# Hybrid encoder on one core: one more feed-forward chunk as seven products, shared PSUM banks, wider weight sums, and x kept in DRAM during the FFN

## The chip, the cores and the metric

The kernel runs on one core of one Trainium2 chip, in one launch. The metric is device time in microseconds (us), lower is better. The kernel before was run three times: 1098.07, 1098.73 and 1100.32 us, median 1098.73 us. One further execution was profiled; it took 1098.06 us. Engine names are those of the profile: PE (TensorE matmuls), PEld (its weight loads), DVE (VectorE), ACT (ScalarE), POOL (GpSimd), SP (SyncE, here a queue of DMA issues).

## What is computed

A residual trunk of two layers on 512 tokens of width 1024, all in float32. Layer 0 mixes tokens by a bidirectional gated linear attention (GLA), layer 1 by grouped-query softmax attention; each is followed by a gated feed-forward network (FFN) with a depthwise convolution of width 3 over the tokens:

```python
for i in range(DEPTH):
    h = rmsnorm(x, norm_mix[i])
    x = x + (gla_mixer(h, ...) if i % 2 == 0 else attn_mixer(h, ...))
    x = x + conv_ffn(rmsnorm(x, norm_ffn[i]), ...)

def conv_ffn(h, w_up, w_conv, b_conv, w_down):
    u = h @ w_up                                # 512 x 1024 by 1024 x 5632
    u = depthwise_conv_width_3(u, w_conv) + b_conv
    val, gate = split(u, 2)
    return (silu(gate) * val) @ w_down          # 512 x 2816 by 2816 x 1024
```

The change is in the FFN, which runs twice with the same code, and in what the FFN shares with the rest (temporaries, x).

## The kernel before, in words

**Layout.** x is held transposed, as eight tiles of 128 features by 512 tokens. Every matrix product in full precision is three float32r matmuls: a number is split into a high part (its rounding to float32r, by a copy on ACT) and a low part (the rest, by a subtraction on DVE), and high*high, high*low and low*high are added up in PSUM. So each 128x1024 weight piece costs one ACT copy (L227) and one DVE subtraction (L228) beside its load; activations are split in the same way. Where a tile is split "by DMA" (`low_dma`, L178) ACT makes both the high part and the negated high part, and a DMA of POOL's queue (L217, in `flush`) adds the original to it, so that DVE has nothing to do.

**Weights.** `Weights` holds the list of all pieces in the order of use (`todo`). `piece` hands out one and makes the next ones ahead of use, `UPA` or `PA` pieces (3 and 4); `make` splits a piece into a `wh` and a `wl` tile, of which there are four each (`NH`, `NL`), and `load` issues the DMA on SP into one of four `raw` tiles, `LOADS` (3) keys ahead.

**The up-projection** runs over 22 chunks m; each gives 128 features of val (t=0) and 128 of gate (t=1). A plain chunk (`plain_up`) has two tiles of 8 x 3 = 24 matmuls of 512 columns (L387 to L389 under `mm3`), 48 in all. The chunks of `SEVEN` (twelve of them: 7, 8, 10-13, 15, 16, 18-21) treat the chunk as a 2x2 block product (inputs even/odd k, tokens in two halves of 256) by seven instead of eight block products (a Strassen-Winograd scheme). A block product is 4 pairs x 3 = 12 matmuls of 256 columns (L857), so a chunk has 84. `seven_up` writes out the order of the products and of the ACT copies and DVE additions between them: product 1 goes to r1; ACT copies r1 to r2 (L873), product 6 adds to r2; ACT copies r2 to r3 (L877), products 7, 3, 5 and 4 follow, then product 1 of the next chunk (`begin_up`), then product 2. The results go to SBUF temporaries c and d of tag `u` by L885 to L894. Four weight quarters are loaded per such chunk and combined by `summed` into seven operands in four pieces; `PLACE` says which piece holds which product's weight.

**The convolution** (`act_up`, L904 to L909) takes one ACT and two DVE passes per tile, then silu and the product. In the first `SWITCH` (4) chunks the input is only scaled by the norm's weight, and a DVE pass per tile (L845) multiplies by the row norms R; after that the inputs are `fresh`, eight tiles rescaled by `rescale` and split by DMA. The sums and differences of the inputs for the seven products are made by `prepare_input` after the chunks in `INPUT_AT`.

**The down-projection.** Every two chunks `prepare` makes the seven inputs of one pair p for the down product (q, differences, then four splits into `gu` tiles); for p in `Q_DMA` (2, 4, 5, 6) the splits go by DMA. After chunks 9 and 17 (`DOWN_AFTER`) `down_part` multiplies eight chunks by their down weights, again by seven products for each of four output pairs n; its results f and g are added to x in SBUF by DMAs of POOL's queue. The last six chunks follow at the end as plain matmuls ("dn"), and `end` adds them to x on DVE (L1008).

**Order.** Each engine runs its instructions in the order in which the tile framework's planner has put them, which follows the program's order where operands and buffers are ready by its own estimate of times. A tile of a tag waits until one of that tag's buffers is free. PSUM has eight banks: acc 3, s 2, pt 2, po 1.

Of the kernel before, what the change touches and what calls it, by code (L numbers as in the profile page):

```python
# [48 lines left out]
SEVEN = (7, 8, 10, 11, 12, 13, 15, 16, 18, 19, 20, 21)  # L49
# [3 lines left out]
SWITCH = 4  # L53
INPUT_AT = {3: (0, 1), 4: (2,), 5: (3,)}
Q_DMA = (2, 4, 5, 6)
NR = 4
NH = 4
NL = 4

# [9 lines left out]
def hybrid_encoder_kernel(  # L69
# [25 lines left out]
    pp = ctx.enter_context(tc.tile_pool(name="pp", bufs=1, space=bass.MemoryType.PSUM))  # L95

# [17 lines left out]
    def tmp(tag, n, w=S):  # L114
        return sp.tile([P, w], F32, tag=tag, bufs={"u": 4, "t": 6, "sq": 3}[tag], name=nm(n))
# [5 lines left out]
    x = [cp.tile([P, S], F32, name=f"x{c}") for c in range(KC)]  # L121
    prm = cp.tile([P, PC_N], F32, name="prm")

    class Weights:
# [3 lines left out]
        def __init__(self):  # L128
            self.todo, self.made, self.by_dma, self.pending = [], {}, [], []
            self.sums, self.last, self.fine = set(), None, []  # L130
            self.loaded, self.strip = {}, {}

        def add(self, src, strips=None, pieces=2):
            for i in strips or range(src.shape[0]):
                order = (0, 1, 3, 2) if pieces > 2 and src.shape[0] == FC else range(pieces)
                self.todo += [(src, i, h) for h in order]
                if pieces > 2:
                    self.sums.add((id(src), i))
# [22 lines left out]
        def make(self, key):  # L161
# [7 lines left out]
            if any(src is a and i < n for a, n in self.by_dma):  # L169
                self.low_dma(hi, lo, r)  # L170
            else:
# [3 lines left out]
        def two(self):  # L175
            return pair("wh", NH, F32R, "wh"), pair("wl", NL, F32R, "wl")

        def low_dma(self, hi, lo, r):  # L178
            act.activation(hi, r, AF.Copy)
            act.activation(lo, r, AF.Copy, scale=-1.0)  # L180
            self.pending.append((lo, r))

        def summed(self, src, i, h):
# [3 lines left out]
            a21, a11, a12, a22 = t1[:, :S], t1[:, S:], t3[:, :S], t3[:, S:]  # L187
            if h == 0:
                r = tmp("t", "sum")
                with tc.issue_after(self.last.ins) if self.last else ExitStack():  # L190
                    dve.tensor_tensor(r, a21, a11, ALU.add)
                    dve.tensor_tensor(a21, a21, a22, ALU.add)
                hi, lo = self.two()
                for sl, y in ((slice(0, S), r), (slice(S, 2 * S), a11)):
                    act.activation(hi[:, sl], y, AF.Copy)
                    dve.tensor_tensor(lo[:, sl], y, hi[:, sl].bitcast(F32), ALU.subtract)
                return hi, lo
            if h == 1:
                dve.tensor_tensor(a11, a21, a11, ALU.add)
                hi, lo = self.two()  # L200
                self.split(hi, lo, t1)
                return hi, lo
            if h == 2:
                hi, lo = self.two()
                self.split(hi, lo, t3)
                return hi, lo
            r = tmp("sq", "sum4")
            dve.tensor_tensor(r, a11, a12, ALU.add)
            hi, lo = (sp.tile([P, S], F32R, tag="sq", bufs=3, name=nm(n)) for n in ("wh4", "wl4"))
            act.activation(hi, r, AF.Copy)  # L210
            self.last = dve.tensor_tensor(lo, r, hi.bitcast(F32), ALU.subtract)
            return hi, lo

        def flush(self):

            for lo, r in self.pending:
                pool.dma_start(lo.bitcast(F32), r, accum_op=ALU.add)  # L217
# [23 lines left out]
        def ahead(self, n):  # L241
# [3 lines left out]
            for key in self.todo[:LOADS]:  # L245
# [36 lines left out]
    act.dma_start(prm, par)  # L282
    raw = [pair("raw", NR, F32, "first") for i in range(4)]
# [145 lines left out]
    def out_steps(src, hl, nxt, late):  # L429
# [19 lines left out]
        def end(ng):  # L449
            for n in range(2):  # L450
                c = ng * 2 + n
                dve.tensor_tensor(x[c], x[c], pss[ng][n], ALU.add)
                nxt.chunk(c)

# [10 lines left out]
    def gla(norm, nxt):  # L465
# [58 lines left out]
        rst = sp.tile([P, S], F32R, tag="t", bufs=6, name="rst")  # L524
# [77 lines left out]
        def f32r(tag, n):  # L602
            return sp.tile([P, S], F32R, tag=tag, bufs={"u": 4, "t": 6}[tag], name=nm(n))
# [770 lines left out]
```

## Time and profile before

| | |
|---|---|
| median of three runs | 1098.73 us (1098.07 to 1100.32) |
| profiled execution | 1098.06 us |
| its span, first to last instruction | 1096.3 us |
| around the span | 1.8 us |
| granted TensorE clock | 1.000 |

The FFN of layer 0 takes the span's 227 to 583 us, the attention layer 583 to about 747, the FFN of layer 1 to the end. In the FFN of layer 0, plain chunks run to 298 us, chunks 7 and 8 to 324, chunk 9 and the first down part to 375, chunks 10 to 13 to 415, chunk 14, 15, 16 and 17 to 460, the second down part to 500, chunks 18 to 21 to 540, the plain down matmuls to 583.

How to read the views: the page gives each engine's busy time; "windows" gives it by stage; "lines" groups instructions of one kind with their mean duration; the timeline gives start, length, engine, line, what is written and read, and in brackets the idle time before and what ended it. A matmul's recorded duration is longer than the distance to the next one, since matmuls are pipelined: the cost of a matmul in a stream is the distance from start to start. The same holds, by less, for DVE and ACT: a row "x2" is two instructions that overlap a little.

### The profile page before, as it was taken

How to read it: one execution, taken by the hardware profiler on the slowest of the kernel's cores; microseconds unless marked ns; L12 is line 12 of the kernel's file. 1: busy time of each engine (PE TensorE's matmuls, PEld its weight loads, DVE VectorE, ACT ScalarE, POOL GpSimd, SP SyncE). 2: the span in 40 equal slices, each digit the busy share in tenths (PEclk: the TensorE clock that was granted, in tenths of full speed). 3: DMA queues.
4: the chain of work that ended last, by engine and by line, in shares of the span. 5: the costliest groups of instructions: out<-in, count | busy, mean ns of one | idle time of the engine just before them, and what ended most of it. 6: DMA issues, size and time to landing. Idle time of an engine off the chain costs nothing.

```text
span 1096.3 us, 17577 instructions
## 1 busy us (share of the span) xinstructions
PE 1088.7 (99%) x6644; PEld 975.0 (89%) x6644; DVE 881.3 (80%) x1417; ACT 678.0 (62%) x1158; POOL 143.4 (13%) x158
## 2 busy tenths in 40 slices
PE   9999999999999999999999999999999999999998
PEld 7888888888899999999988888788889999999997
DVE  6686776669989799988955588766998979998892
ACT  6565343447766677666764677745776667766670
POOL 0100123000100211010014343000110021101000
PEclk9999999999999999999999999999999999999999
DMA  7432223236645745364457474433673574536422
GB/s 255 132 98 95 66 70 116 83 101 162 154 111 140 174 121 149 116 164 125 154 137 180 120 227 143 157 111 97 157 163 103 147 171 124 146 111 166 125 95 77
DMA packets 52309, 146.45 MB, mean 134 GB/s; under 512 B 6144, under 2 KB 7680, under 8 KB 52224
## 3 DMA queue, kind: packets, MB, share of 16 engines
q1 hardware_dynamic: 32736, 102.17, 28.5%
q0 software_dynamic: 14592, 34.61, 17.2%
q10 hardware_dynamic: 4896, 8.55, 2.1%
q8 instruction: 52, 0.85, 0.3%
q14 instruction: 33, 0.27, 0.1%
HBM read 100.21 MB, written 2.10 MB: 93 GB/s over the span
## 4 chain that ended last, share of the span: by engine, by line
PE 94%; DVE 2%; ACT 2%; issue 1%; DMA 1%; DVEq 0%; SPq 0%; ACTq 0%
PE r L857 33%; PE vg L419 8%; PE op L445 8%; PE up L387 7%; PE up L388 7%; PE up L389 7%; PE dn L387 2%; PE dn L388 2%; PE dn L389 2%; PE av L419 1%; PE o L713 1%; PE A L387 1%; PE B L387 1%; PE A L389 1%; PE B L389 1%
## 5 line engine op out<-in xcount | busy, mean ns | idle before, releaser
L227 ACT ACTIVATE wh<-raw 128x1024 fp32r<-128x1024 f32 x164 | 171.6, 1055 | 146.7 <-PE op L445 32.1
L228 DVE TENSOR_TENSOR wl<-raw,wh 128x1024 fp32r<-128x1024 f32 x164 | 199.9, 1224 | 46.4 <-ACT wh L227 43.5
L857 PE MATMUL r<-gu,wh 128*128 128x256 f32 x896 | 162.8, 284 | 0.0
L857 PE MATMUL r<-xt,wh 128*128 128x256 f32 x768 | 141.1, 284 | 1.0 <-ACT r L873 1.0
L857 PEld LDWEIGHTS r<-gu,wh 128*128 128x128 f32 x896 | 140.1, 192 | 1.6 <-ACT r L976 0.6
L857 PE MATMUL r<-gu,wl 128*128 128x256 f32 x448 | 126.5, 283 | 0.0
L857 PEld LDWEIGHTS r<-xt,wh 128*128 128x128 f32 x768 | 119.9, 192 | 2.6 <-ACT r L873 1.8
L857 PE MATMUL r<-xt,wl 128*128 128x256 f32 x384 | 108.3, 283 | 0.0
L857 PEld LDWEIGHTS r<-gu,wl 128*128 128x128 f32 x448 | 85.9, 192 | 0.0
L857 PE MATMUL r<-nl,wh 128*128 128x256 f32 x288 | 81.5, 283 | 0.0
L857 PE MATMUL r<-nh,wl 128*128 128x256 f32 x288 | 81.5, 283 | 0.0
L857 PE MATMUL r<-nh,wh 128*128 128x256 f32 x288 | 81.5, 283 | 0.0
L419 PE MATMUL vg<-wh,xhl 128*128 128x512 f32 x256 | 79.7, 390 | 1.1 <-DVE wh L225 1.1
L387 PE MATMUL up<-nh,wh 128*128 128x512 f32 x192 | 74.9, 390 | 0.0
L388 PE MATMUL up<-nl,wh 128*128 128x512 f32 x192 | 74.9, 390 | 0.0
L389 PE MATMUL up<-nh,wl 128*128 128x512 f32 x192 | 74.7, 389 | 0.0
L857 PEld LDWEIGHTS r<-xt,wl 128*128 128x128 f32 x384 | 73.5, 192 | 0.0
L445 PE MATMUL op<-oT,wh 128*128 128x512 f32 x256 | 72.1, 394 | 0.0
L419 PEld LDWEIGHTS vg<-wh,xhl 128*128 128x128 f32 x256 | 48.0, 188 | 11.2 <-ACT sq L361 1.3
L445 PEld LDWEIGHTS op<-oT,wh 128*128 128x128 f32 x256 | 47.4, 188 | 9.7 <-ACT oT L741 0.3
L857 PEld LDWEIGHTS r<-nl,wh 128*128 128x128 f32 x288 | 55.3, 192 | 0.2
L857 PEld LDWEIGHTS r<-nh,wh 128*128 128x128 f32 x288 | 55.3, 192 | 0.2
(279 smaller groups left out, 2745.2 us busy)
## 6 DMA issues: line engine op xcount, KB each, us to landing
raw<-in_w_up_dram SPq DMA_DIRECT2D x84, 512.0 KB, 3.9
raw<-in_w_down_dram SPq DMA_DIRECT2D x44, 512.0 KB, 4.1
wl<-raw POOLq DMA_DIRECT2D x16, 512.0 KB, 4.9
raw<-in_w_vg_dram SPq DMA_DIRECT2D x12, 512.0 KB, 3.9
ring<-p ACTq DMA_DIRECT2D x22, 256.0 KB, 2.9
raw<-in_w_kq_dram SPq DMA_DIRECT2D x8, 512.0 KB, 3.6
raw<-in_w_gout_dram SPq DMA_DIRECT2D x8, 512.0 KB, 3.6
nl<-xr POOLq DMA_DIRECT2D x8, 512.0 KB, 5.3
```

Of the source, the lines that this page charges most:

```text
L227: act.activation(hi[:, sl], r[:, sl], AF.Copy)
L228: dve.tensor_tensor(lo[:, sl], r[:, sl], hi[:, sl].bitcast(F32), ALU.subtract)
L387: mm(ps, wh, mh, start=start, stop=False)
L388: mm(ps, wh, ml, start=False, stop=False)
L389: return mm(ps, wl, mh, start=False, stop=stop)
L419: mm(ps[j][:, :width], hl[k][i == 2][:, j * P : (j + 1) * P], (wl if i == 1 else wh)[:, sl], start=k == 0 and i == 0, stop=k == KC - 1 and ...
L445: mm(pss[ng][n], wt[:, sl], mv, start=k == 0 and i == 0, stop=k == KC - 1 and i == 2)
L713: last = mm(og[s], l, r, start=False, stop=i == len(parts) - 1, skip_group_check=True)
L857: mm(dst, w[:, sl], m, start=start and j == 0 and a == 0, stop=j == len(pairs) - 1 and a == 2, skip_group_check=True)
```

## The change

- Chunk 6 joins `SEVEN`. `SWITCH` and `INPUT_AT` come one chunk earlier. The weights of chunk 5 are split by DMA (`UP_DMA`); no pair of the down inputs is any more (`Q_DMA` is empty).
- `seven_up` and `down_part`: r1 and r2 are the two halves of one bank (`both`). Product 1 goes to a bank of tag pt, and one ACT operation writes it to both halves. The order is 1, 6, 7, 4, 5, then product 1 of the next, 2, 3 (before: 1, 6, 7, 3, 5, 4, next 1, 2). r3 gets r2 twice, before product 4 into its left half and after product 5 into its right half; one addition of 512 columns (`add_seven`) replaces two or three of 256. The convolution of t=0 reads `both` from PSUM.
- The signs of the sums change so that the sums need no negation. The four weight quarters are loaded in another order, and `summed` makes two sums by one operation of 1024 columns into a `raw` tile.
- x is made of four pair tiles with a tag. After the mixer each pair is stored to DRAM (`x_save`, on SP), the down parts' DMAs add to it there, and it is loaded again at chunk 20 (`x_load`). Between chunks 1 and 20 every third weight piece goes into the x tiles (`two`), and `PAW` = 6 pieces are made ahead instead of 4.
- `raw` has five tiles instead of four; the temporaries `u` have three instead of four, `t` five instead of six. In the attention the fourth rotary temporary takes the tile `R`, and all six copies of the probabilities take `wh`, `wl` and `raw` tiles.

```diff
-SEVEN = (7, 8, 10, 11, 12, 13, 15, 16, 18, 19, 20, 21)
+SEVEN = (6, 7, 8, 10, 11, 12, 13, 15, 16, 18, 19, 20, 21)
-SWITCH = 4
-INPUT_AT = {3: (0, 1), 4: (2,), 5: (3,)}
-Q_DMA = (2, 4, 5, 6)
-NR = 4
+SWITCH = 3
+INPUT_AT = {2: (0, 1), 3: (2,), 4: (3,)}
+Q_DMA = ()
+UP_DMA = (5,)
+NR = 5
+LOADS_FFN = 3
+WIDE_AT, BACK_AT = 1, 20
+PAW, UPAW = 6, 3
...
-    x = [cp.tile([P, S], F32, name=f"x{c}") for c in range(KC)]
+    def x_tiles():
+        tiles = [pair("x", KC // 2, F32, "x") for p in range(KC // 2)]
+        x[:] = [t[:, i * S : (i + 1) * S] for t in tiles for i in range(2)]
+        return tiles
+    def x_save(p):
...
+            sync.dma_start(x_home[p][:, i * S : (i + 1) * S], x[2 * p + i])
+    def x_load():
+        for home, t in zip(x_home, x_tiles()):
+            sync.dma_start(t, home)
...
         def two(self):
+            self.turn += self.wide
+            if self.wide and self.turn % 3 == 0:
+                return pair("x", KC // 2, F32R, "wh"), pair("x", KC // 2, F32R, "wl")
             return pair("wh", NH, F32R, "wh"), pair("wl", NL, F32R, "wl")
...
         def summed(self, src, i, h):
             t1, t3 = self.strip[id(src), i][:2]
-            a21, a11, a12, a22 = t1[:, :S], t1[:, S:], t3[:, :S], t3[:, S:]
...
+            a11, a21, a12 = t1[:, :S], t3[:, :S], t3[:, S:]
+            if h == 3:
+                del self.strip[id(src), i]
+                r = a12
+                dve.tensor_tensor(r, a12, a21, ALU.subtract)
+                hi, lo = (sp.tile([P, S], F32R, tag="sq", bufs=3, name=nm(n)) for n in ("wh4", "wl4"))
+                act.activation(hi, r, AF.Copy)
+                self.last = dve.tensor_tensor(lo, r, hi.bitcast(F32), ALU.subtract)
                 return hi, lo
             if h == 1:
+                e = pair("raw", NR, F32, "sum")
+                self.strip[id(src), i].append(e)
+                both = lambda t: t.rearrange("p (o n) -> p o n", n=S)
+                with tc.issue_after(self.last.ins) if self.last else ExitStack():
+                    dve.tensor_tensor(both(e), both(a21).to_broadcast([P, 2, S]), both(t1), ALU.subtract)
+                dve.tensor_tensor(a21, a11, e[:, S:], ALU.subtract)
+            hi, lo = self.two()
+            self.split(hi, lo, self.strip[id(src), i][h])
             return hi, lo
...
         def seven_up(m):
-            r1 = bank("acc", "r1")[:, :H]
-            go(1, r1, True)
-            r2 = bank("acc", "r2")[:, :H]
-            act.activation(r2, r1, AF.Copy)
+            r = bank("pt", "r1")[:, :H]
+            go(1, r, True)
+            both = bank("acc", "r")
+            r1, r2 = both[:, :H], both[:, H:]
+            twice(both, r)
             yield
             go(6, r2, False)
-            r3 = bank("s", "r3")[:, :H]
-            act.activation(r3, r2, AF.Copy)
+            r3 = bank("s", "r3")
+            act.activation(r3[:, :H], r2, AF.Copy)
             r4 = bank("pt", "r4")[:, :H]
             go(7, r4, True)
-            r5 = bank("pt", "r5")[:, :H]
-            go(3, r5, True)
+            d = tmp("u", "u")
+            twice(d, r4)
+            go(4, r3[:, :H], False)
             go(5, r2, False)
...
+            act.activation(r3[:, H:], r2, AF.Copy)
+            add_seven(d, r3, r4)
+            yield 1, d
             begin_up(m + 1)
             go(2, r1, False)
...
+            go(3, r2, False)
+            yield 0, both
...
+        def twice(d, r4):
+            two = lambda a: a.rearrange("p (o t) -> p o t", t=H)
+            act.activation(two(d), two(r4).to_broadcast([P, 2, H]), AF.Copy)
+        def add_seven(d, r3, r4):
+            dve.tensor_tensor(d, d, r3, ALU.add)
...
-        PLACE = {1: (0, S), 7: (0, 0), 6: (1, S), 5: (1, 0), 2: (2, 0), 4: (2, S), 3: (3, 0)}
+        PLACE = {1: (0, 0), 4: (0, S), 6: (1, 0), 2: (1, S), 7: (2, 0), 5: (2, S), 3: (3, 0)}
...
         held = []
         for m in range(FC):
+            if m == BACK_AT:
+                W.loads, W.wide = LOADS, 0
+                x_load()
+            elif m == WIDE_AT:
+                W.loads, W.wide = LOADS_FFN, 1
             held.append(act_up(m))
```

`down_part` gets the same order and the same shared bank, with g = both copied by one ACT operation of 512 columns in place of two of 256, and its DMAs add to `x_home` in place of x.

More of the change, by code (lines that the diff above doesn't have):

```diff
@@ L131, in __init__ @@
             self.loaded, self.strip = {}, {}
+            self.loads, self.wide, self.turn = LOADS, 0, 0
         def add(self, src, strips=None, pieces=2):
             for i in strips or range(src.shape[0]):
-                order = (0, 1, 3, 2) if pieces > 2 and src.shape[0] == FC else range(pieces)
-                self.todo += [(src, i, h) for h in order]
+                self.todo += [(src, i, h) for h in range(pieces)]
                 if pieces > 2:
@@ L170, in make @@
                 self.low_dma(hi, lo, r)
+            elif any(src is a and i in UP_DMA for a in up):
+                self.low_dma(hi, lo, r)
             else:
@@ L244, in ahead @@
                 n -= 1
-            for key in self.todo[:LOADS]:
+            for key in self.todo[: self.loads]:
                 self.load(key)
@@ L850, in product @@
             if h not in pieces:
-                pieces[h] = W.piece(src, strip, h, PA)
+                pieces[h] = W.piece(src, strip, h, PAW if W.wide else PA)
             wh, wl = pieces[h]
```

118 lines of the change are left out of this document (43 added, 75 removed).

## The prediction

> **What bounds the kernel now.** I read the page first, then the chain, then the windows of the FFN, then the rows of single operations.
>
> ```profile
> span 1096.3 us, 17577 instructions
> PE 1088.7 (99%) x6644; PEld 975.0 (89%) x6644; DVE 881.3 (80%) x1417; ACT 678.0 (62%) x1158; POOL 143.4 (13%) x158
> PE 94%; DVE 2%; ACT 2%; issue 1%; DMA 1%; DVEq 0%; SPq 0%; ACTq 0%
> ```
>
> PE is on the chain for 94% of the span. So time falls only where PE has less to do, or where it waits; and an engine that runs late costs time only when its lateness reaches PE. The price of a matmul is its distance to the next (the chain and PE's timeline; start, length):
>
> ```profile
> 305.08 18.71 PE r L857 x156
> 460.22 79.84 PE r L857 x660
> 272.18 0.39 PE L387 MATMUL up<-nh,wh 128*128 128x512 f32 x1
> 281.70 0.39 PE L387 MATMUL up<-nh,wh 128*128 128x512 f32 x1
> ```
>
> The 256-column products come every 18.71/156 = 0.120 us (0.121 over the longer stretch). The two plain rows are 42 matmuls apart: 9.52/42 = 0.2267 us. A seven-product chunk is 84 x 0.1205 = 10.12 us, a plain one 48 x 0.2267 = 10.88 us.
>
> DVE is the engine behind (columns of the windows: length, then busy time of PE, PEld, DVE, ACT, POOL):
>
> ```profile
> 239.00:329.00 90.00, 90.00 (x478) 77.94 (x477) 84.45 (x140) 63.14 (x92) 10.44 (x12) 1.00 0.57 139
> 329.00:375.00 46.00, 46.00 (x361) 44.82 (x360) 40.57 (x60) 29.56 (x50) 6.86 (x8) 1.00 0.62 155
> 375.00:465.00 90.00, 89.47 (x657) 85.20 (x657) 85.68 (x139) 66.63 (x120) 10.48 (x13) 1.00 0.51 134
> ```
>
> In the first stretch (to the end of chunk 8) DVE has 5.6 us to spare, in the second 5.4, in the third (chunks 10 to 17) 4.3. PE's one real wait in the FFN lies in the third:
>
> ```profile
> PE r L857 <- ACT r L873: 1.0, 2, 0.5
> ...
> 409.79 0.28 PE L857 MATMUL r<-nh,wl 128*128 128x256 f32 x1
> 410.60 0.50 PE L857 MATMUL r<-xt,wh 128*128 128x256 f32 x2 [0.53 <-ACT r L873]
> ...
> 408.62 0.40 ACT L179 ACTIVATE gu<-b 128x256 fp32r<-128x256 f32 x1
> 409.24 1.04 ACT L227 ACTIVATE wh<-raw 128x1024 fp32r<-128x1024 f32 x1
> 410.19 0.36 ACT L873 ACTIVATE r<-r 128x256 f32<-128x256 f32 x1
> ```
>
> The matmul after 409.79 should start at 409.91 and starts at 410.60: 0.69 us late, because the copy of r1 to r2 stands on ACT behind splits by DMA (L179, L180) and a weight copy. It happens twice, once a layer: 1.4 us.
>
> **The change, part by part.** Sums are against the profiled execution's 1098.06 us, which is 0.67 us (0.06%) under the median; I make no correction for that.
>
> *Chunk 6* removes 10.88 and adds 10.12 us of PE: 0.76 a layer, **-1.5 us**. [...]
>
> *DVE.* I price an operation by its step in a row of two (row's length less one duration):
>
> ```profile
> 344.04 2.35 DVE L228 TENSOR_TENSOR wl<-raw,wh 128x1024 fp32r<-128x1024 f32 x2
> 241.42 1.28 DVE L845 TENSOR_TENSOR u<-up,R 128x512 f32<-128x512 f32 x2
> 252.18 0.74 DVE L948 TENSOR_TENSOR xr<-xr 128x256 f32<-128x256 f32 x2
> 254.23 1.41 DVE L906 SCALAR_TENSOR_TENSOR y<-u,cw,y 128x511 f32<-128x511 f32 x2
> L228 DVE TENSOR_TENSOR wl<-raw,wh 128x1024 fp32r<-128x1024 f32 x164 | 199.9, 1224 | 46.4 <-ACT wh L227 43.5 <-issue 1.3 <-PE r L857 1.3
> ```
>
> 1024 columns: 2.35 - 1.22 = 1.13 us; 512: about 0.60; 256: 0.33; the convolution's 511: 0.66. A strip's weights took two wide and seven 512 operations, 6.46 us; now four wide and three 512, 6.32. The chunk's combination was three of 256 (0.99), now one of 512 (0.60). So a seven chunk saves 0.53, a down output 0.2. A pair no longer split by DMA costs three of 512 and one of 256: +2.13. Chunk 5's weights by DMA: -2.26. One chunk less to multiply by R: -1.2. Chunk 6 as seven: 6.32 + 0.60 - 2.26 = +4.66. Per stretch and layer: first +4.7 - 1.1 - 2.3 - 1.2 + 2.1 (pair 2) = +2.2, and PE is 0.76 shorter, so 5.6 to spare becomes 2.6; second 5.4 becomes 6.2; third, six chunks and pairs 4, 5, 6: -3.2 + 6.4 = +3.2, so 4.3 becomes 1.1. DVE is then 97 to 99% busy in two stretches, and still has room. The two more pieces made ahead (about 1.9 us of DVE each) let it take 3 to 4 us of the third stretch's work into the second. I cost DVE at nothing for the sum; if that cover fails, what it lacks goes to PE one for one.
>
> *ACT* loses three negated copies of 512 and one of 256 for each of four pairs (rows L179, L180), about 1.9 us a pair, and that is what stood ahead of the late copy. Besides, product 6 now follows product 1 after two products (2 and 3), 2.9 us, instead of one, so the widened copy has twice the cover: the 0.69 us wait goes, **-1.4 us**. What is late next is the other copy (rival 1).
>
> *The copy r2 to r3.* Before, products 7, 3 and 5 lay between product 6 and product 4, which needs it (and 7 and 3 ahead of 5, which overwrites r2); now product 7 alone, 1.44 us, less the copy's 0.37 and about 0.15 of signalling: it may begin 0.9 us after product 6. Rows of three chunks (PE's product 6 and the product after it, in chunk 12 the one after it alone, in chunk 15 product 6 at the head of a row of the chain; then the copy, L877):
>
> ```profile
> 376.63 0.40 PE L857 MATMUL r<-xt,wh 128*128 128x256 f32 x2
> 378.07 0.40 PE L857 MATMUL r<-xt,wh 128*128 128x256 f32 x2
> 381.67 0.37 ACT L877 ACTIVATE r<-r 128x256 f32<-128x256 f32 x1
> 398.39 0.40 PE L857 MATMUL r<-xt,wh 128*128 128x256 f32 x2
> 399.77 0.36 ACT L877 ACTIVATE r<-r 128x256 f32<-128x256 f32 x1
> 428.96 18.89 PE r L857 x156
> 432.90 0.36 ACT L877 ACTIVATE r<-r 128x256 f32<-128x256 f32 x1
> ```
>
> It began 3.6 us after product 6 in chunk 10, 1.4 in chunk 12, and 2.5 in chunk 15 (product 6 from 428.96, 12 x 0.12 long, so to 430.40). With the new order that is 2.7 + 0.5 + 1.6 = 4.8 us a layer. But in chunks 10 and 15 the splits of a pair, six and more operations, stood ahead of it, and these are now half. The bounds are 0 and 9.6 us; I take **+0.6**, nearer to none.
>
> *GLA temporaries.* With three `u`, the low part of the attention matrix (L659) must wait for one of the state's matmuls (kv) to be done; before it was made ahead of them:
>
> ```profile
> 118.33 0.69 DVE L659 TENSOR_TENSOR atl<-at,ath 128x512 fp32r<-128x512 f32 x1 [0.70 <-ACT ath L658]
> 120.09 1.23 DVE L228 TENSOR_TENSOR wl<-raw,wh 128x1024 fp32r<-128x1024 f32 x1 [0.17 <-ACT wh L227]
> 119.97 0.28 PE L389 MATMUL kv<-vrh,ktl 128*128 128x256 f32 x1
> 121.40 0.28 PE L702 MATMUL o<-vrh,atl 128*128 128x256 f32 x1
> ```
>
> Its buffer is free at about 120.3 and PE wants it at 121.40: in time if DVE takes it at once, 0.5 us late if it comes behind the weight split that ends at 121.3. Three heads: 0 to 1.5 us; I take **+0.4**.
>
> *DMAs.*
>
> ```profile
> raw<-in_w_up_dram SPq DMA_DIRECT2D x84, 512.0 KB, 3.9
> x<-f POOLq DMA_DIRECT2D x16, 256.0 KB, 5.9
> xt<-xr POOLq DMA_DIRECT2D x8, 512.0 KB, 5.1
> 296.47 0.86 POOL L217 DMA_DIRECT2D xt<-xr  x1 [10.14 <-DVE y L906]
> ```
>
> Eight stores of x and four loads a layer join SP's queue, and the down parts' additions go to DRAM, which no row shows. The stores wait for x's addition on DVE, with weight loads behind them that are three keys (some 15 us) early against 3.9. The loads at chunk 20 wait for x tiles that hold weights of chunks 20 and 21 at most, until about 540; two plain down pieces (5.4 us of PE each) are loaded before them. An addition to DRAM that took twice 5.9 us would still be done long before: the second part's f is made by 500, x is next used after 550. I cost these at nothing. The inputs xt of chunk 6 are needed a chunk earlier; the last was issued at 296.5, landed some 5 us later and was used from 305, so 3 us lay between, and the work before it moves up too. In the attention, the same number of tiles serves the copies and the probabilities: nothing.
>
> *Sum:* -1.5 - 1.4 + 0.6 + 0.4 = -1.9; 1098.06 - 1.9 = **1096.2 us**, 0.23% under the median.
>
> **Rivals.** (1) *The r3 copy is late* in the chunks that begin a run of sevens or follow a pair's splits: PE stops before product 4. For it: the rows above, a cover cut from three products to one, and in-order ACT. Against it: in the down part the cover was one product already (7 before 5), and the stretch from 460.22 shows 0.121 us per matmul. Price up to 9.6 us: 1098.06 - 2.5 + 9.6 = 1105.2; half of it, 1100.4. It decides for slower from 5.3 us on (55% of it). Centre 1102.
> (2) *DVE is full.* The spare 2.6 and 1.1 us are lost to waits of DVE on ACT (43.5 us of idle time before L228 over the span). If PE gets 1.0 us late in each of the two stretches of each layer: 1096.2 + 4 - 1.0 (the copy's and GLA's cost then hidden in it) = 1099.2, within the bound.
> (3) *More goes than I count.* The longer row of products takes 0.121 us where the shorter takes 0.120: over the page's 3360 such matmuls 3.5 us, in small pieces, 1.4 of it the wait above. If most of the rest, 1.5 us, goes too, with weights made earlier, and neither cost comes: 1098.06 - 1.5 - 1.4 - 1.5 = 1093.7.
> (4) *Nothing of the wait goes*, it only moves, and the GLA costs 1.0: 1098.06 - 1.5 + 1.0 = 1097.6.
> (5) *A wait by bank.* Product 2 writes the half of `both` beside the one that ACT still copies to r3 after product 5; product 1 of the next chunk, 1.44 us, lies between. If PE is held until that copy is done, the L877 delays above would cost at most the same 4.8 us a layer, 9.6 in all; I take half: 1098.06 - 1.9 + 4.8 = 1101.0. The traces so far show no matmul held by a read of another half of its bank, and r1 and r2 had a bank each, so nothing here bears on it. [...]
>
> **How the numbers follow.** 0.2% of the median is 2.2 us, about what a measurement can tell from no change: faster is below 1096.5, slower above 1100.9. Forecast 0.42 (own range 1094.7 to 1097.5), of which 0.36 faster; rival (1) 0.21, all but 0.02 slower; (2) 0.16, of which 0.03 slower; (3) 0.10, faster; (4) 0.06, the same; (5) 0.05, slower. Faster 0.46, same 0.27, slower 0.27. The range runs from 1093.5 to 1103.5: it leaves out the upper part of rivals (1) and (5), about 0.1, and the ends of (3), about 0.05.
>
> **What would show it.** Right: 84 more L857 matmuls and 48 fewer "up" per layer, at 0.120 us; no wait on the widened copy; L877's successor beginning within 0.9 us of product 6; DVE at 97% or more in both stretches. Wrong: gaps of PE before product 4 released by ACT (rival 1); gaps before product 1 or 6 with weights as releaser, and DVE without idle time ahead of them (2); idle PE at the o matmuls of the GLA of over 0.5 us a head; any stall at 294 us (xt), or at 550 and the end, where x comes back from DRAM.

## The result and the profile after

The changed kernel took 1097.34 us (median of 20 runs, 1096.08 to 1099.39), the kernel before, run beside it, 1099.81 us (20 runs). The ratio is 0.9981, with a 95% interval of 0.9975 to 0.9987: some 2.1 us faster (the medians are 2.5 us apart). A ratio of 1 lies outside the interval, but the gain is just under the 0.2% from which the prediction calls a kernel faster. Outside the span the kernel before took 1.7 or 1.8 us in each execution beside the experiments; the changed one took 2.2 to 2.9 us in 6 of its 20 executions, and why is not known. The profiled execution of the changed kernel took 1098.02 us, with a span of 1096.3 us and a granted clock of 0.999. Its line numbers are new: the product matmul is L878, the copies to r3 L899 (left half) and L906 (right half), the widened copy L933, the weight copy and split L246 and L247.

The page's head and chain:

```profile
span 1096.3 us, 17372 instructions
PE 1088.1 (99%) x6716; PEld 977.2 (89%) x6716; DVE 879.6 (80%) x1309; ACT 675.3 (62%) x1078; POOL 119.6 (11%) x130
PE 95%; DVE 2%; ACT 1%; DMA 1%; issue 1%; SPq 0%; DVEq 0%; ACTq 0%
```

There are 72 matmuls more, 36 a layer: 84 product matmuls in place of 48 plain ones. What else PE waited for is in the waits view (engine and line, what released it; total, times, longest):

```profile
PE r L878 <- ACT r L906: 0.7, 1, 0.7
PE pt L1256 <- DMA ring<-p: 0.5, 1, 0.5
PE o L723 <- DVE atl L680: 0.3, 2, 0.2
```

The wait on the copy of r1 to r2 (1.0 us in two) is gone. Four small ones have come: one in the FFN, one in the attention, two in the GLA.

The windows of the three stretches of layer 0's FFN, each set to end with the same work as before:

```profile
241.00:330.00 89.00, 88.80 (x509) 78.06 (x509) 86.11 (x134) 67.56 (x94) 8.72 (x10) 1.00 0.57 142
330.00:376.00 46.00, 46.00 (x357) 44.68 (x356) 40.63 (x54) 29.47 (x47) 5.22 (x6) 1.00 0.56 134
376.00:465.00 89.00, 89.00 (x658) 84.93 (x657) 85.92 (x121) 60.45 (x94) 1.73 (x2) 1.00 0.37 109
```

DVE is 97% busy in the first and the third (86.11 and 85.92 of 89), as forecast, and PE is busy in all of the third. ACT has fallen from 66.63 to 60.45 us there. The chain has

```profile
338.56 76.46 PE r L878 x636
```

which is 0.120 us a product matmul (76.46/636), where the longer rows of before had 0.121.

To compare kernels I cut each trace at fixed matmuls: the GLA runs from the ninth vg matmul to the first "up", each FFN from its first "up" to its last "dn", the attention from there to the next "up" (us, starts of matmuls). The cut after the eighth vg matmul leaves most of the start out, of which more at the end (in e12_q2_layer1 the GLA still holds 0.5 us of it).

| profiled run | GLA | FFN 0 | attention | FFN 1 |
|---|---|---|---|---|
| before | 217.84 | 346.46 | 173.65 | 346.49 |
| changed | 218.74 | 344.79 | 174.08 | 345.27 |
| e1_six_plain | 218.92 | 346.02 | 173.82 | 345.83 |
| e2_two_banks | 218.71 | 344.97 | 173.87 | 345.19 |
| e3_atl_t | 217.24 | 344.63 | 173.81 | 345.31 |
| e4_no_wide | 218.71 | 348.01 | 173.97 | 348.05 |
| e5_before_six | 217.87 | 352.60 | 173.77 | 347.63 |
| e6_old_q | 218.75 | 347.59 | 173.75 | 345.37 |
| e8_dve_copy | 218.65 | 348.25 | 174.58 | 348.00 |
| e9_q2 | 217.29 | 346.08 | 173.83 | 344.47 |
| e10_paw5 | 217.26 | 345.05 | 174.04 | 344.84 |
| e11_no_up_dma | 218.70 | 345.43 | 174.10 | 345.43 |
| e12_q2_layer1 | 217.76 | 344.65 | 173.79 | 344.85 |
| e13_warm | 217.32 | 344.76 | 174.41 | 344.45 |

The change: GLA +0.90, FFN 0 -1.67, attention +0.43, FFN 1 -1.22, together -1.56 us. How far a single profile can be trusted is shown by e13_warm: it differs from e10_paw5 by three matmuls at the start alone, and yet its FFNs are 0.29 and 0.39 us shorter and its attention is 0.37 us longer. Differences of that size in this table prove nothing by themselves.

**The wait by bank** is seen in layer 1, chunk 7. PE, then ACT in the changed kernel:

```profile
832.50 0.28 PE L878 MATMUL r<-nh,wl 128*128 128x256 f32 x1
832.61 0.42 PE L878 MATMUL r<-xt,wh 128*128 128x256 f32 x2
833.75 0.39 PE L878 MATMUL r<-nh,wh 128*128 128x256 f32 x1 [0.71 <-ACT r L906]
833.97 0.28 PE L878 MATMUL r<-nl,wh 128*128 128x256 f32 x1
```

```profile
830.47 1.06 ACT L246 ACTIVATE wh<-raw 128x1024 fp32r<-128x1024 f32 x1 [1.22 <-DVE raw L228]
831.44 1.04 ACT L246 ACTIVATE wh<-sum 128x1024 fp32r<-128x1024 f32 x1
832.38 1.04 ACT L246 ACTIVATE wh<-raw 128x1024 fp32r<-128x1024 f32 x1
833.33 0.37 ACT L906 ACTIVATE r<-r 128x256 f32<-128x256 f32 x1
```

The row at 832.50 ends product 1 of chunk 8, two matmuls of its product 7 follow (the planner put them there), and at 833.75 begins product 2 of chunk 7, when ACT's copy of r2 is done. Product 2 writes r1, the other half of that bank; product 3, which overwrites r2, comes 12 matmuls later. The copy is late since three weight copies stand ahead of it on ACT, the first of which waited 1.22 us for DVE. From 832.75 (the second of the pair) to 833.75 are 1.00 us instead of 0.12, and from there to 833.97 0.22: a stop cost 0.10 us more at the matmul after it, here and at the other stops of over 0.12 us ahead of a product in these traces (0.22 us each time; the stop of 4.2 us in the last section cost more), so 0.98 us in all. Layer 0 has the same stop, which costs 0.33 us in all.

**In the GLA**, the changed kernel:

```profile
121.64 1.23 DVE L247 TENSOR_TENSOR wl<-raw,wh 128x1024 fp32r<-128x1024 f32 x1 [0.17 <-ACT wh L246]
122.78 0.69 DVE L680 TENSOR_TENSOR atl<-at,ath 128x512 fp32r<-128x512 f32 x1
123.07 0.28 PE L723 MATMUL o<-vrl,ath 128*128 128x256 f32 x1
123.52 0.39 PE L723 MATMUL o<-vrh,atl 128*128 128x256 f32 x1 [0.17 <-DVE atl L680]
123.74 0.28 PE L723 MATMUL o<-vrh,ath 128*128 128x256 f32 x1
```

The low part comes behind the weight split, where it stood before it in the old kernel; 0.33 + 0.10 us are lost, and as much at 143 us.

### The profile page after: what moved, and what is told of

It reads as the page before. It is cut to its first block, busy times and chain, and to the rows that moved or that the text cites. A ratio compares the mean times of both kernels' runs of the same rounds, so it can differ in the third digit from the quotient of the medians.

```text
span 1096.3 us, 17372 instructions
## 1 busy us (share of the span) xinstructions
PE 1088.1 (99%) x6716; PEld 977.2 (89%) x6716; DVE 879.6 (80%) x1309; ACT 675.3 (62%) x1078; POOL 119.6 (11%) x130
## 4 chain that ended last, share of the span: by engine, by line
PE 95%; DVE 2%; ACT 1%; DMA 1%; issue 1%; SPq 0%; DVEq 0%; ACTq 0%
PE r L878 36%; PE vg L439 8%; PE op L465 8%; PE up L408 6%; PE up L409 6%; PE up L407 6%; PE dn L408 2%; PE dn L407 2%; PE dn L409 2%; PE av L439 1%; PE o L734 1%; PE A L407 1%; PE A L409 1%; PE B L409 1%; PE B L407 1%; PE A L408 1%
## 5 line engine op out<-in xcount | busy, mean ns | idle before, releaser
L246 ACT ACTIVATE wh<-raw 128x1024 fp32r<-128x1024 f32 x160 | 166.8, 1053 | 115.5 <-PE op L465 32.1
L247 DVE TENSOR_TENSOR wl<-raw,wh 128x1024 fp32r<-128x1024 f32 x160 | 194.8, 1219 | 40.5 <-ACT wh L246 40.4
L878 PE MATMUL r<-gu,wh 128*128 128x256 f32 x896 | 161.9, 283 | 0.0
L878 PE MATMUL r<-xt,wh 128*128 128x256 f32 x832 | 151.3, 283 | 0.1
L878 PEld LDWEIGHTS r<-gu,wh 128*128 128x128 f32 x896 | 140.2, 192 | 0.8
L878 PEld LDWEIGHTS r<-xt,wh 128*128 128x128 f32 x832 | 130.0, 192 | 0.9 <-ACT r L899 0.6
L878 PE MATMUL r<-gu,wl 128*128 128x256 f32 x448 | 126.6, 283 | 0.0
L878 PE MATMUL r<-xt,wl 128*128 128x256 f32 x416 | 117.4, 283 | 0.0
L878 PE MATMUL r<-nh,wh 128*128 128x256 f32 x312 | 89.0, 285 | 0.8 <-ACT r L906 0.7
L878 PE MATMUL r<-nh,wl 128*128 128x256 f32 x312 | 88.3, 283 | 0.0
L878 PE MATMUL r<-nl,wh 128*128 128x256 f32 x312 | 88.3, 283 | 0.0
L878 PEld LDWEIGHTS r<-gu,wl 128*128 128x128 f32 x448 | 85.9, 192 | 0.0
L878 PEld LDWEIGHTS r<-xt,wl 128*128 128x128 f32 x416 | 79.7, 192 | 0.0
L878 PEld LDWEIGHTS r<-nh,wh 128*128 128x128 f32 x312 | 59.8, 192 | 3.4 <-ACT r L906 3.0
L878 PEld LDWEIGHTS r<-nl,wh 128*128 128x128 f32 x312 | 59.8, 192 | 0.2
L878 PEld LDWEIGHTS r<-nh,wl 128*128 128x128 f32 x312 | 59.8, 192 | 0.0
```

Of the source, the lines that this page charges most:

```text
L246: act.activation(hi[:, sl], r[:, sl], AF.Copy)
L247: dve.tensor_tensor(lo[:, sl], r[:, sl], hi[:, sl].bitcast(F32), ALU.subtract)
L878: mm(dst, w[:, sl], m, start=start and j == 0 and a == 0, stop=j == len(pairs) - 1 and a == 2, skip_group_check=True)
```

## The experiments

All runs were timed beside the kernel before in five rounds; ratios are to it. Where a kernel differs from the changed one, only the edit is shown.

### Which part brings what

**e1_six_plain**

```diff
-SEVEN = (6, 7, 8, 10, 11, 12, 13, 15, 16, 18, 19, 20, 21)
+SEVEN = (7, 8, 10, 11, 12, 13, 15, 16, 18, 19, 20, 21)
```

> The changed kernel with chunk 6 plain again (SWITCH and INPUT_AT stay early, all else stays changed). My theory: the 2.1 us that the change gained are 1.5 from chunk 6 and 1.4 from the wait on the widened copy, less some 0.8 paid back in the GLA, and less the two copies that come late in chunks 6 to 8 (0.9 and 0.3 us in one layer, 0.3 in the other). Without chunk 6 there are 72 matmuls fewer, 1.5 us more of PE work, but DVE has 4.7 us a layer less to do just there, so the late copies should go too: 0.2 to 1.5 us over the changed kernel, I say 0.6, so 1097.9 against 1099.8 of before. Rival A (chunk 6 is the whole gain, the wait's removal is paid back elsewhere): within 0.4 us of before, 1099.5 or so. Rival B (the gain is the order and the earlier weights, and chunk 6 gains nothing because DVE then is late): no more than 0.2 us from the changed kernel.

Measured: 1099.29 us, ratio 0.9999 (0.9990 to 1.0007). This is rival A: without chunk 6 nothing is left. By the table the FFNs are 0.44 and 0.66 us shorter than before, the GLA is 1.08 longer. Copies to r3 are late here too, at another place (waits view):

```profile
PE r L878 <- ACT r L899: 0.8, 2, 0.6
```

**e5_before_six**: the kernel before with chunk 6 alone.

```diff
-SEVEN = (7, 8, 10, 11, 12, 13, 15, 16, 18, 19, 20, 21)
+SEVEN = (6, 7, 8, 10, 11, 12, 13, 15, 16, 18, 19, 20, 21)
-SWITCH = 4
+SWITCH = 3
-INPUT_AT = {3: (0, 1), 4: (2,), 5: (3,)}
+INPUT_AT = {2: (0, 1), 3: (2,), 4: (3,)}
```

> The kernel before with chunk 6 as seven products and nothing else (SWITCH and INPUT_AT one chunk earlier). Theory: PE has 0.73 us a layer less to do, and DVE 4 us a layer more in the stretch to the end of chunk 8, of which 5.6 were spare; the wait on the copy of r1 to r2 in chunk 13 stays, since neither the order nor ACT's splits changed: 0 to 1.5 us faster than before, I say 1.0, 1098.1, and the rest of the change is needed for the other half. Rival: DVE gets late by what PE saves or more, so chunk 6 is only to be had with the cheaper sums: no faster than before, or up to 3 us slower.

Measured: 1105.73 us, ratio 1.0067 (1.0053 to 1.0080), slower than either had it (the rival allowed for up to 3 us). Its waits view and POOL's row in the timeline, then the same row of the changed kernel:

```profile
PE r L857 <- DMA xt<-xr: 5.2, 2, 4.2
...
PE r L857 <- ACT r L873: 1.1, 2, 0.5
...
292.08 0.86 POOL L217 DMA_DIRECT2D xt<-xr  x1 [12.33 <-ACT xt L180]
```

```profile
288.34 0.86 POOL L236 DMA_DIRECT2D xt<-xr  x1 [7.72 <-ACT xt L206]
```

The last input of chunk 6 was issued at 292.1, landed 7.6 us later, and PE wanted it at 295.3: 4.35 us lost, and 1.13 in layer 1. In the changed kernel it is issued at 288.3, lands in 5.2 us, and is wanted after 297. The wait on r1 to r2 stays (the second row). So chunk 6 alone is a loss; the cheaper sums, the order and the DMA split of chunk 5 earn their keep by letting it in.

**e11_no_up_dma**: the last of these three taken back.

```diff
-UP_DMA = (5,)
+UP_DMA = ()
```

> The changed kernel with chunk 5's weights split on DVE again. Chunk 6 as seven in the kernel before stopped PE for 4.4 and 1.1 us, since its last input arrived late (DVE made the sums 5 us later than in the changed kernel, and ACT and the DMA followed). Theory: DVE's time ahead of these sums decides, and this DMA split is what keeps it: DVE gets 2.3 us more per layer, the last input's DMA is issued some 2 us later, of 4 us in hand, so there is no stop on it, but the copies of chunks 6 to 8 come later: 1 to 4 us slower than the changed kernel, I say 2, 1099.3. Rival: the cheaper sums and the new order carry chunk 6 alone: within 0.5 us of the changed kernel.

Measured: 1097.74 us, ratio 0.9993 (0.9984 to 1.0002); FFNs 0.64 and 0.16 us longer than the changed kernel's. The last input is issued 2.1 us later, as I said, and there is now a stop on it (0.37 and 0.30 us), which I had denied: less was in hand than 4 us. A second stop waits for a weight that DVE splits (0.47 and 0.36 us), and the ones on L906 are gone. By the ratios this kernel is some 1.3 us slower than the changed one, by the FFNs 0.8, and the intervals of the two ratios overlap; that lies between the rival and what I said. Against the loss of e5_before_six it is little: the sums and the order carry most of it.

### The waits on ACT's copies

**e2_two_banks**

```diff
-            both = bank("acc", "r")
-            r1, r2 = both[:, :H], both[:, H:]
-            twice(both, r)
+            r1, r2 = bank("acc", "r")[:, :H], bank("acc", "r")[:, :H]
+            act.activation(r2, r, AF.Copy)
+            act.activation(r1, r, AF.Copy)
...
-            go(3, r2, False)
-            yield 0, both
+            c = tmp("u", "u")
+            act.activation(c[:, :H], r1, AF.Copy)
+            go(3, r2, False)
+            act.activation(c[:, H:], r2, AF.Copy)
+            yield 0, c
```

> The changed kernel with r1 and r2 of an up chunk in two banks again (two ACT copies of 256 instead of the widened one, and two ACT copies into a temporary c that the convolution reads). The order of the products is unchanged, and the down part too. If product 2 is held by the bank (the copy from the right half of the bank that it writes), the row of the waits view with the right copy to r3 as the releaser goes away, 0.9 us in layer 1 and 0.3 in layer 0; ACT has 0.9 us more per chunk, which should show as later copies to r3 in a few places: between 1.2 us faster and 1.5 us slower than the changed kernel, I say 0.3 faster, 1097.0. Rival: product 2 was late for another reason (its weights, or the sequence on PE): the same stop of 0.7 to 0.9 us ahead of product 2 of chunk 7 stays.

Measured: 1098.10 us, ratio 0.9988 (0.9979 to 0.9997); the FFNs are within 0.2 us of the changed kernel's. Here the copy is as late (ACT), and PE runs through it. Product 2 begins at 831.05, ahead of the copy at 831.26:

```profile
830.32 1.04 ACT L246 ACTIVATE wh<-raw 128x1024 fp32r<-128x1024 f32 x1
831.26 0.36 ACT L906 ACTIVATE r<-r 128x256 f32<-128x256 f32 x1
```

```profile
830.93 0.28 PE L878 MATMUL r<-nh,wl 128*128 128x256 f32 x1
831.05 0.28 PE L878 MATMUL r<-nh,wh 128*128 128x256 f32 x1
831.17 0.28 PE L878 MATMUL r<-nl,wh 128*128 128x256 f32 x1
```

It is these rows that show the cause, and not the missing stop: that is missing in e11_no_up_dma and e10_paw5 too, where the bank is shared. The edit separates two things at once, since r1 and r2 shared not only a bank but a tile of the program. A tile alone did not hold PE at another place: at the start of the changed kernel ACT writes the second half of a `wh` tile at 7.99 us,

```profile
7.99 0.62 ACT L246 ACTIVATE wh<-first 128x512 fp32r<-128x512 f32 x1
```

and PE has been reading its first half since 6.04 us (row in the last section). That tile lies in SBUF; for a tile in PSUM no run tells bank and tile apart.

But nothing is won: with two copies more per chunk on ACT, the copy to r3's left half is late in four places:

```profile
PE r L878 <- ACT r L899: 0.9, 4, 0.3
```

**e6_old_q**

```diff
-Q_DMA = ()
+Q_DMA = (2, 4, 5, 6)
```

> The changed kernel with the splits of pairs 2, 4, 5 and 6 by DMA again. What took the wait on the widened copy away in chunk 13: the cover of two products (then it stays away here), or ACT's missing splits (then it is back, 0.7 us a layer). Theory: the cover; but ACT's splits now stand ahead of the copies to r3, which have one product of cover, so PE stops ahead of product 4 in chunks 10, 12 or 15: 1 to 4 us slower than the changed kernel, I say 2, 1099.3. Rival: ACT's splits were harmless, and DVE, with 8.5 us a layer less to do, is no longer late in chunks 6 to 8: 0.5 to 1.5 us faster than the changed kernel.

Measured: 1100.07 us, ratio 1.0012 (1.0004 to 1.0021). The FFNs are 2.9 us longer than the changed kernel's, where I said 2, and nearly all of it is in layer 0 (+2.80; FFN 1 +0.10, where the stop of chunk 15 has come, 0.77 us, and the one of 0.98 us on L906 has gone). Two of the stops of layer 0 show it. In chunk 7 of layer 0 the widened copy stands behind eight splits, of which the last rows are

```profile
307.87 0.40 ACT L205 ACTIVATE gu<-b 128x256 fp32r<-128x256 f32 x1
308.17 0.40 ACT L206 ACTIVATE gu<-b 128x256 fp32r<-128x256 f32 x1
308.48 0.58 ACT L933 ACTIVATE r<-r 128x512 f32<-128x512 f32 x1
```

```profile
309.11 0.50 PE L878 MATMUL r<-xt,wh 128*128 128x256 f32 x2 [0.76 <-ACT r L933]
...
437.03 0.50 PE L878 MATMUL r<-xt,wh 128*128 128x256 f32 x2 [0.61 <-ACT r L899]
```

and at 437 the copy to r3 in chunk 15 is late behind pair 6's. In chunk 13, where the old wait was, there is none. So the longer cover is enough there, but it is no safeguard: with a pair's splits ahead of it the widened copy is late all the same. Fewer splits without the longer cover were not run.

**e8_dve_copy** (in the up chunks)

```diff
-            act.activation(r3[:, H:], r2, AF.Copy)
+            dve.tensor_copy(r3[:, H:], r2)
```

> The changed kernel with the copy of r2 to the right half of r3 on DVE instead of ACT, in the up chunks. If ACT's queue (weight copies that wait for DVE) is what makes that copy late in chunk 7, the row with ACT as releaser goes. But DVE gets 13 x 0.33 us a layer more, 2 us in the third stretch, where I had put its spare time at 1.1, and the copy then stands behind weight splits of 1.13 us, ahead of product 2: 1 to 5 us slower than the changed kernel, I say 2.5, 1099.8. Rival (DVE has room, its 97% is only the look of early work): within 0.5 us of the changed kernel or faster.

Measured: 1105.26 us, ratio 1.0055 (1.0042 to 1.0067); FFNs +3.46 and +2.73. The ACT row on L906 is gone, but new ones add up to more. 13 copies, priced by estimate at the 0.33 us step of a 256-column operation in the kernel before, are 4.3 us a layer on DVE, and PE pays 3.1 of them (the mean of the two FFNs), so DVE has no room for them, against the rival. Its waits view and third stretch:

```profile
PE up L407 <- ACT u L933: 1.3, 1, 1.3
...
PE up L407 <- DVE y L923: 0.8, 1, 0.8
```

```profile
376.00:465.00 89.00, 87.72 (x636) 82.55 (x635) 84.30 (x121) 56.12 (x84) 1.58 (x2) 1.00 0.35 104
```

**e4_no_wide**

```diff
-WIDE_AT, BACK_AT = 1, 20
+WIDE_AT, BACK_AT = 99, 20
```

> The changed kernel in which the tiles of x never hold weights (four wh and wl tiles, four pieces ahead, as before; x still goes to DRAM and back). Theory: DVE is 97% busy in two stretches and lives on work made ahead; with four pieces it can take less of a crowded stretch's work into an easy one, so PE gets stops released by weights (wh, wl) in chunks 10 to 17: 1 to 4 us slower than the changed kernel, I say 2, 1099.3. Rival (the depth is worth nothing, DVE's spare time is enough): within 0.4 us of the changed kernel.

Measured: 1103.91 us, ratio 1.0039 (1.0027 to 1.0052): 3.22 and 2.78 us more in the FFNs, above my range. The releasers are the weights, as I said:

```profile
PE r L878 <- ACT wh L246: 1.0, 4, 0.3
PE r L878 <- DVE wl L247: 0.4, 2, 0.2
```

DVE's work is that of the changed kernel. What is missing is the work made ahead.

### Towards a better version

**e3_atl_t**

```diff
-            hi, lo = f32r("u", "ath"), f32r("u", "atl")
+            hi, lo = f32r("u", "ath"), f32r("t", "atl")
```

> The changed kernel with the low part of the attention matrix of the GLA in a temporary of tag t instead of u. Theory: the two stops of 0.43 us each ahead of the o matmuls (about 123 and 143 us of the span) come from the third u, and go: 0.7 to 0.9 us faster than the changed kernel, 1096.5. Rival: the low part is late because DVE is behind there anyhow (values and weight splits), and the stops stay or move to another operation: no change, 1097.3.

Measured: 1094.90 us, ratio 0.9962 (0.9949 to 0.9974). The two stops go, and the GLA is 1.50 us shorter than in the changed kernel, 0.60 less even than before. The 0.6 us are a further stop, which both kernels have (here the changed one's row), on a chain of DVE work that came behind a weight split at 181 us and is put before it here:

```profile
188.84 0.53 PE L758 MATMUL tp<-ident,gr 128*128 128x128 f32 x4 [0.25 <-DVE g L748]
```

The next three start from e3_atl_t.

**e9_q2**

```diff
-Q_DMA = ()
+Q_DMA = (2,)
```

> The kernel with atl in tag t (1094.9 us, against 1099.1 of before), and in it the splits of pair 2 by DMA again. They lie in the stretch to chunk 8: DVE gets 2.1 us a layer less there, ACT 1.9 more, in chunks 5 and 6. Theory: the right copy to r3 is late in chunk 7 since ACT's weight copies wait for DVE, so its stops (0.97 and 0.32 us) get smaller by half or more: 0.3 to 1.3 us faster, I say 0.8, 1094.1. Rival: ACT's extra splits stand ahead of copies to r3, and the time is the same or up to 1 us more.

Measured: 1096.95 us, ratio 0.9978 (0.9969 to 0.9987). Theory and rival both came, one in each layer. Against e3_atl_t, FFN 1 is 0.84 us shorter, and the stop of chunk 7 is gone; FFN 0 is 1.45 us longer, with the widened copy and copies to r3 late as in e6_old_q.

**e12_q2_layer1**

```diff
-Q_DMA = ()
+Q_DMA = (2,)
...
-            far = p in Q_DMA
+            far = p in Q_DMA and layer == 1
```

> The kernel with atl in tag t, and pair 2's splits by DMA in layer 1 alone, where the profile of the run with both layers had the FFN 0.8 us shorter and no stop behind those splits (in layer 0 it was 1.4 us longer). Theory (the stops of a layer follow from the program's order and come back): 0.6 to 1.0 us faster than with atl alone, 1094.1. Rival (that difference was chance): the same as with atl alone, 1094.9, or slower.

Measured: 1095.70 us, ratio 0.9973 (0.9963 to 0.9983). A miss: FFN 1 is 0.46 us shorter, not 0.84, with a new stop of 0.41 us ahead of a product that waits for r3. The stop moved with the order around it.

**e10_paw5**

```diff
-PAW, UPAW = 6, 3
+PAW, UPAW = 5, 3
```

> The kernel with atl in tag t, and in it five weight pieces ahead instead of six. The right copy to r3 in chunk 7 stood behind three weight copies on ACT that were made ahead of need; with one piece less ahead, fewer stand there: its stop (0.97 us in layer 1) gets smaller, but the reserve against DVE's full stretches shrinks (with four pieces and no tiles of x the cost was 6.0 us in two layers). Theory (the reserve is worth most): 0 to 2 us slower than with six, I say 0.8, 1095.7. Rival (six is more than is needed): 0.3 to 1.3 us faster, 1094.0.

Measured: 1094.56 us, ratio 0.9962 (0.9953 to 0.9972). Against e3_atl_t, FFN 0 +0.42, FFN 1 -0.47: neither the theory nor the rival, and little more than a stage varies by. The stop on L906 is gone in both layers, and one on L899 has come in both. Five pieces do; this and e3_atl_t are the best versions found, some 4 us under before and 2 under the changed kernel.

**e13_warm**, from e10_paw5, a question of the start (last section):

```diff
+    for i in range(3):
+        mm(warm[:, P : 2 * P], two[:, :P], two[:, P : 2 * P], start=True, stop=True)
```

> The kernel with atl in tag t and five pieces ahead, and three more warm-up matmuls at the start (into another part of the same PSUM tile, read by nobody), so that PE has no pause of 1.1 us ahead of its first product. Times of every kernel here lie in two groups, 1.6 us and more apart, and the profiles of the later group show the first eight vg matmuls at half rate (3.5 us against 1.9). Theory: the clock rises when PE has been busy without the pause for long enough, so the pause is what lets some executions begin cold; with it filled the later group goes or comes within 1 us: median 1094.2, nothing above 1096. Rival (the rise depends on when the launch falls, not on the pause): two groups as before, median 1094.6 and some runs above 1096.5.

Measured: 1096.47 us, ratio 0.9975 (0.9966 to 0.9985), in two groups: five runs from 1094.7 to 1095.8, five from 1097.2 to 1098.3. Two groups are what the rival said; its reason, when the launch falls, no run shows.

## Why the prediction was nearly right, point by point

The forecast was 1096.2 us, and the changed kernel took 1097.3. The start of the sum makes that miss: 1098.06 us was one execution of the kernel before, 1.75 us under the median of its 20 runs, and from that median the same sum gives 1097.9. The forecast sum was -1.9 us, the profile's -1.56, the ratio's some -2.1. The sum held because misses of both signs, each up to 1.7 us, happened to balance: that part is luck. "Stops" are distances from start to start beyond 0.120 or 0.227 us, the 0.10 after each stop included.

| term | forecast | found |
|---|---|---|
| chunk 6, PE's work | -1.5 | -1.63 |
| wait on r1 to r2 | -1.4 | -1.56 |
| other small stops of the FFNs | 0 | -1.66 |
| copy to r3, left half (L899) | +0.6 | +0.40 |
| copy to r3, right half, by bank (L906) | 0 | +1.31 |
| GLA | +0.4 | +0.90 |
| attention | 0 | +0.43 |

The row on chunk 6 is 48 x 0.227 less 84 x 0.120 us, twice. The second column adds up to -1.9, the third to -1.81; the cuts give -1.56, and the rest is what the nominal distances round off (many are a few ns shorter, and these are not counted).

*Chunk 6.* Right in size (in each layer 480 matmuls of 512 columns became 432, and 1680 of 256 became 1764, at the distances forecast). Costing DVE's part at nothing was right only in this company. I argued that the inputs come early enough since "the work before it moves up too"; e5_before_six shows that in the old order they do not, and e11_no_up_dma that even here only the DMA split of chunk 5 keeps a stop away.

*The wait on r1 to r2* went, and with its 0.10 us after the stop was worth a little more. I gave two reasons, fewer splits and more cover. By e6_old_q the cover alone ends this wait and lets another come in chunk 7; what fewer splits alone would do was not run.

*The other small stops* are rival (3), "more goes than I count", which I had priced at 1.5 and given 0.10: beside the wait, the FFNs of before had 1.66 and 1.70 us of stops, the changed ones beside those on L899 and L906 0.73 and 0.97. It was there, and so were the costs that this rival left out.

*The copy to r3's left half* was late once, in layer 0 (0.30 and 0.10 us): the lower part of my bounds was right. The 0.15 us of signalling in its cover is about what the trace of the kernel before shows: 0.10 from the end of product 1's last matmul (499.51 us) to ACT's copy (L873 at 499.61), and 0.05 from that copy's end (410.55) to PE (410.60). Rival (1), its 5 us and more, did not come, but e6_old_q brings its mechanism back in chunk 15.

*The wait by bank*, rival (5), is the step that failed: I had it at nothing in the sum and at 0.05 as a rival, because no row of before showed such a wait. It could not: r1 and r2 had a bank each. It happened in one chunk a layer, 0.33 and 0.98 us, and e2_two_banks shows that their sharing one bank (as halves of one tile) is its cause. My cover argument (product 1 of the next chunk, 1.44 us) failed where ACT was behind by three weight copies (830.47 to 833.33 us in layer 1).

*The GLA's* mechanism was right to the instruction (the low part behind the weight split, 0.43 us against 0.5 a head), its size was off by two: it happened in two heads of the three, where my +0.4 stood for less than one.

*The attention* I put at nothing. PE waited 0.5 us on a copy to the ring in the changed kernel, 0.2 to 0.9 in its variants, but 0.3 in e5_before_six too, which has the old ring; the stage is 0.1 to 0.9 us longer than before in all of them. Whether the new place of the third pair of copies does it or chance was not tried.

*The DMAs* at nothing held in the FFN: the waits view shows none of PE there that a DMA ended. *DVE* at nothing was right, and rival (2) did not come; e8_dve_copy and e4_no_wide show how near it was: by estimate 4.3 us a layer more on DVE, or four pieces of reserve for six, cost 3 us a layer.

## What to carry to other kernels

Here an engine that was 97% busy was harmless only with work made ahead: with that reserve cut (e4_no_wide), or a third of a microsecond more per chunk (e8_dve_copy, by estimate 4.3 us a layer), some 3 us a layer reached the engine that sets the time. Two results that shared a PSUM bank, as halves of one tile, were one resource for the program's waits: ACT's late read of one half kept PE from writing the other for 0.98 us in layer 1 and 0.33 in layer 0. So count every read of either half against every write of the other, and give it the cover that the slowest queue needs. And a part that brings nothing by itself (here all but chunk 6) may be what makes another part possible, so undo parts one by one in both kernels, the old one too.

## What was not expected of the hardware

**A stop of 4.2 us cost more than its length.** In e5_before_six, after the 4.2 us wait, PE ran at half rate for some 5 us. Its windows, two in the stop and one after it (the third figure from the end is the granted clock), and PE's timeline:

```profile
295.60:297.70 2.10, 0.00 (x0) 0.00 (x0) 1.27 (x2) 0.00 (x0) 0.00 (x0) 1.00 0.88 195
297.75:299.70 1.95, 0.00 (x0) 0.00 (x0) 0.00 (x0) 0.00 (x0) 0.00 (x0) 0.50 0.18 36
299.60:304.50 4.90, 4.77 (x22) 4.77 (x23) 2.96 (x6) 2.49 (x6) 0.00 (x0) 0.50 0.00 0
```

```profile
299.73 0.58 PE L857 MATMUL r<-xt,wh 128*128 128x256 f32 x1 [4.19 <-DMA xt<-xr]
300.11 0.42 PE L857 MATMUL r<-xt,wl 128*128 128x256 f32 x1
300.33 0.42 PE L857 MATMUL r<-xt,wh 128*128 128x256 f32 x1
```

After the stop the clock is 0.50 and the distance 0.21 us instead of 0.12; over 22 matmuls that is another 2 us. The wait of 1.0 us in layer 1 had no such sequel: it cost 1.13 us in all. The granted clock went to 0.50 at 297.7 us, when PE had been idle for 2.2 us (the last matmul before the stop ends at 295.5), and is back, at 0.99 over the window from 304.5 to 309.5, in which 44 matmuls ran in 5.0 us; that is 4.8 us after PE began again. This is one stop of one execution; what sets the two times no run shows.

**Times lie in two groups, 1.6 us apart in the kernel before.** Nine of its 20 runs beside the changed kernel took 1098.07 to 1099.07 us, eleven 1099.65 to 1100.61 (medians 1098.49 and 1100.10). The times of e1_six_plain, e10_paw5, e12_q2_layer1 and e13_warm have a gap too, of 1.1 to 1.5 us; those of the changed kernel run into one another, but its spans are 1094.2 to 1095.1 us in eleven executions and 1095.8 to 1097.3 in nine. The start has such a difference: the first vg matmuls of the changed kernel's profile, and those of e3_atl_t's.

```profile
6.04 2.04 PE L439 MATMUL vg<-wh,xhl 128*128 128x512 f32 x4 [0.97 <-DVE wh L244]
7.89 1.85 PE L439 MATMUL vg<-wl,xhl 128*128 128x512 f32 x4
```

```profile
6.09 1.16 PE L439 MATMUL vg<-wh,xhl 128*128 128x512 f32 x4 [1.33 <-DVE wh L244]
7.09 1.09 PE L439 MATMUL vg<-wl,xhl 128*128 128x512 f32 x4
```

Eight matmuls take 3.5 us in the one and 1.9 in the other, though the same 16 warm-up matmuls stand before them, in rows of 3.78 and 3.47 us (the profile's clock reads 1.00 over the longer start too, so the rate is read from the distances alone). What makes the two starts differ no trace shows. Filling the pause before the first product (e13_warm) did not take the second group away. Of its ten executions the five longer ones have a granted clock of 0.998 and the five shorter ones 0.999 or 1.000, so in that kernel the clock has a part in it; but no profile of a longer one was taken, so what sets its group stays open. For the reader it means that one profiled time of these kernels can be 1.6 us off, the distance of the two groups of before, for no reason of its own: the two profiles compared here come from different groups, so that both have a span of 1096.3 us, and between them only the cuts, which leave out the start, show the gain.
